# Fixed homes, by their address, for the split weights of a two-layer trunk on one core

## The chip, the cores and the metric

One Trainium2 chip, one core. The time is that of one execution in device microseconds (us). The engines are called PE (TensorE), DVE (VectorE), ACT (ScalarE), POOL (GpSimd) and SP (SyncE, which issues nearly all transfers).

## What is computed

Two layers on x of 512 tokens by 1024 channels, all in float32. Each layer is SwiGLU half-step, mixer, SwiGLU half-step; every sub-layer has a norm, a shift and scale from a conditioning vector, and a gated residual. Layer 0 mixes by gated convolutions, layer 1 by pooling and block attention. Cut to what matters here:

```python
def swiglu(h, w_gate, w_up, w_down):
    return (jax.nn.silu(h @ w_gate) * (h @ w_up)) @ w_down

for i in range(DEPTH):
    mod = (cond @ ada_w[i] + ada_b[i]).reshape(bn, N_SUBLAYERS, 3, D_MODEL)
    h = modulate(rms_norm(x, ffn_norm[i, 0]), mod[:, 0, 0], mod[:, 0, 1])
    x = x + 0.5 * mod[:, 0, 2][:, None, :] * swiglu(h, ...)
    h = modulate(rms_norm(x, mix_norm[i]), mod[:, 1, 0], mod[:, 1, 1])
    x = x + mod[:, 1, 2][:, None, :] * (conv_mixers(h, ...) if i % 2 == 0 else pool_moba_mixers(h, ...))
    h = modulate(rms_norm(x, ffn_norm[i, 1]), mod[:, 2, 0], mod[:, 2, 1])
    x = x + 0.5 * mod[:, 2, 2][:, None, :] * swiglu(h, ...)
return rms_norm(x, final_norm)
```

## The kernel before

Everything is kept transposed: channels on the 128 partitions, the 512 tokens along the free dimension. Each float32 operand of a product is split into a high and a low part of the type float32r, and a product of weights w and stream s is three matmuls: high w with high s, high w with low s, low w with high s (`mac`, lines 302 to 304). The streams are hh and hl (the normed input) and th and tl (the hidden values), eight tiles of 512 columns each.

Weights come from HBM by SP into `raw`, a ring of four tiles. `split` (lines 270 to 294) rounds a block of 128 x 1024 into `whi` on ScalarE (line 284) and puts the rest into `wlo`, mostly on VectorE (line 286). whi and wlo are rings of four places, one tag each with four buffers. A few items keep their split weights elsewhere: in th and tl at the start (the joined items), in hh and hl in the two output projections of the mixers (`store`).

Part of gate times up of every SwiGLU is done by pairs of 128 channels with seven products of half width instead of eight (`pair_run`, `seventh`, line 791). These have 256 columns. Per pair: a11 and a12 (weights split by `split_full` into whi, wlo; streams hh, hl), s1 and s3 (also whi, wlo; streams are the sums `f`, tiles f0 to f15), s2 and a22 (weights split by `split_half` into qhi, qlo, line 748; streams f) and s4 (weights qhi, qlo; streams hh, hl). Each is 12 matmuls, so a pair has 84, and there are 56 pairs in 11 runs:

```python
mm(p.hi[name][:, kk, :], xh, first and kk == 0)
mm(p.hi[name][:, kk, :], xl)
mm(p.lo[name][:, kk, :], xh)
```

Between two sub-layers stands a boundary (`boundary`): the last two items of the old one and the first three of the new one are done in halves of 256 columns with whi and wlo, while the norm is computed. All other products have 512 columns.

The order on each engine is written out: a plan of steps is replayed, a split stands at most three items ahead of its use, and takes the place in the ring that was used four splits ago. Memory comes from pools. Constants, streams and x lie in one pool, then raw, the ring, small buffers, and `fp`, which is opened anew for a stage and holds f, q, and all temporaries. Where a tile starts follows from the sizes of those ahead of it. `keep1` (line 844) copies a quarter result into p1c, a buffer of its own in fp.

Of the kernel before, what the change touches and what calls it, by code (L numbers as in the profile page):

```python
# [8 lines left out]
F32 = mybir.dt.float32  # L9
F32R = mybir.dt.float32r  # L10
# [4 lines left out]
P = 128  # L15
D = 1024
S = 512
# [10 lines left out]
W_BUFS = 4  # L28
# [6 lines left out]
class Raw:  # L35


    def __init__(self, shape, src, uses):
        self.shape, self.src, self.uses = shape, src, uses
        self.tile = None  # L40


class Item:


    def __init__(self, raw, cut, shape, post=None, rhs=None, korder=None, store=None):
        self.raw, self.cut, self.shape = raw, cut, shape
        self.post, self.rhs = post, rhs
        self.korder, self.store = korder, store
        self.hi = self.lo = self.ps = None  # L50
        self.left = 0
        self.pool_low = self.late = self.hold = self.by_dma = False


class Pair:
# [13 lines left out]
class Trunk:  # L69
    def __init__(self, ctx, tc, a, out):  # L70
        self.ctx, self.tc, self.nc, self.a, self.out = ctx, tc, tc.nc, a, out
        self.plan = []
        self.later, self.held = [], []
        self.pend = None
        self.ending = False
        self.phase = None
        self.free_banks = list(range(8))
        self.bank_no = {}

# [173 lines left out]
    def load(self, r):  # L253
# [12 lines left out]
        else:  # L266
            r.tile = t.rearrange("p (a b) -> p a b", a=r.shape[1])
            self.nc.sync.dma_start(r.tile, r.src)

    def split(self, it):  # L270
        nk, m = it.shape
        src = it.cut(it.raw.tile)
        if it.store is None:
            parts = [[p.tile([P, 1024], F32R, name=n, tag=n)[:, 0:nk * m].rearrange(
                "p (a b) -> p a b", a=nk) for p, n in ((self.wp, "whi"), (self.wp, "wlo"))]]
            step = nk
        else:
            parts = [[t.rearrange("p (a b) -> p a b", b=m) for t in pair] for pair in it.store]
            step = S // m
        it.hi, it.lo = [], []  # L280
        for i, (hi, lo) in enumerate(parts):
            w = src[:, i * step:(i + 1) * step, :]
            n = w.shape[1]
            self.nc.scalar.copy(hi[:, 0:n, :], w)  # L284
            eng = self.nc.gpsimd if it.pool_low else self.nc.vector
            low = lambda eng=eng, lo=lo, hi=hi, w=w, n=n: eng.tensor_tensor(  # L286
                lo[:, 0:n, :], w, hi[:, 0:n, :].bitcast(F32), op=ALU.subtract)
            if it.by_dma:
                self.nc.scalar.activation(lo[:, 0:n, :], w, AF.Copy, scale=-1.0)
                self.nc.gpsimd.dma_start(lo[:, 0:n, :], w, accum_op=ALU.add)  # L290
            elif it.hold:
                self.held.append(low)
            else:
                low()
            it.hi += [hi[:, a, :] for a in range(n)]
            it.lo += [lo[:, a, :] for a in range(n)]
# [45 lines left out]
    def setup(self):  # L342
        ctx, tc, nc, a = self.ctx, self.tc, self.nc, self.a
# [4 lines left out]
        self.np_ = ctx.enter_context(tc.tile_pool(name="np", bufs=2))  # L348
        self.psum = ctx.enter_context(tc.tile_pool(name="psum", bufs=1, space=PS))
        ctx.enter_context(tc.manual_schedule())  # L350
        cp = self.cp
        self.open_phase()
        rows = lambda n, c, name, i: self.fp.tile([P, S], F32, name=name, tag=SPARE[9 + i], bufs=1)[0:n, 0:c]
# [101 lines left out]
    def open_phase(self):  # L455
        if self.phase is not None:
            self.phase.close()
        self.phase = ExitStack()
        self.fp = self.phase.enter_context(self.tc.tile_pool(name="fp", bufs=2))


    def g_of(self, l, s):
# [104 lines left out]
    def apply(self, i, k, sl, rb):  # L567

        nc = self.nc
        n = sl.stop - sl.start  # L570
        if n == S:
            t = self.fp.tile([P, n], F32, name=f"t{n}", tag="qhi", bufs=3)
        else:
            t = self.np_.tile([P, n], F32, name=f"t{n}", tag="t", bufs=3)
        nc.vector.scalar_tensor_tensor(t, self.x[k][:, sl], self.modA[:, i, k:k + 1],  # L575
                                       rb, op0=ALU.mult, op1=ALU.mult)
        b = self.modB[:, i, k:k + 1]
        nc.scalar.activation(self.hh[k][:, sl], t, AF.Identity, bias=b, scale=1.0)  # L578
        self.low()
        self.pend = lambda: nc.vector.scalar_tensor_tensor(  # L580
            self.hl[k][:, sl], t, b, self.hh[k][:, sl].bitcast(F32), op0=ALU.add, op1=ALU.subtract)

    def low(self):
        fn, self.pend = self.pend, None
        if fn is not None:
            fn()

    def boundary(self, tail, i, head, switch=True):
# [13 lines left out]
        two, third, fourth = head[:2], head[2:3], head[3:4]  # L602
        third[0].late = fourth[0].late = True
        third[0].pool_low = True
        nk = tail[0].shape[0]
        for it in tail:
            self.mm(it, 0)
# [136 lines left out]

    def split_half(self, p, name, src):

        hi, lo = (self.fp.tile([P, S], F32R, name=n, tag=n, bufs=3) for n in ("qhi", "qlo"))
        self.nc.scalar.copy(hi, src)  # L748
        p.hi[name], p.lo[name] = hi.rearrange("p (k c) -> p k c", k=4), lo.rearrange("p (k c) -> p k c", k=4)
        p.lows = getattr(p, "lows", {})  # L750
        p.lows[name] = lambda: self.nc.vector.tensor_tensor(lo, src, hi.bitcast(F32), op=ALU.subtract)  # L751

    def split_full(self, p, names, src):

        hi, lo = (self.wp.tile([P, 1024], F32R, name=n, tag=n) for n in ("whi", "wlo"))
        self.nc.scalar.copy(hi, src)
        for e, n in enumerate(names):
            p.hi[n], p.lo[n] = (t[:, e * S:(e + 1) * S].rearrange("p (k c) -> p k c", k=4) for t in (hi, lo))
        p.lows = getattr(p, "lows", {})
        p.lows[names] = lambda: self.nc.vector.tensor_tensor(lo, src, hi.bitcast(F32), op=ALU.subtract)  # L760
# [63 lines left out]
    def pair_run(self, pairs, down, rest):  # L824
# [16 lines left out]
                self.plan.append(("use", slot))  # L841

        def keep1(p):
            p.p1 = self.fp.tile([P, 256], F32, name="p1c", tag="p1c", bufs=1)
            nc.scalar.copy(p.p1, p.ab[:, 0:256])

        def u2(p):
# [27 lines left out]
        for n, p in enumerate(pairs):  # L875
# [11 lines left out]
            else:  # L887
                self.pre([down[0]])
            product(p, "s2", "x", 2, True)
            do((keep1, p))  # L890
            if r:
                do((low(r, ("a11", "a12")),))
# [30 lines left out]
        p, nf = pairs[-1], down[0].shape[0]  # L923
# [623 lines left out]
    def build(self):  # L1547
        self.setup()
        self.sg, self.rb = {}, {}
        f = {(l, s): self.ffn_items(l, s) for l in range(2) for s in (0, 2)}  # L1550
# [129 lines left out]
        tail = f[1, 2][-1][1][6:]  # L1680
        self.call(lambda: setattr(self, "ending", True))
        self.call(lambda: self.scaled(range(5), FULL))
        for it in tail:
            self.mm(it, 0)
        nk = SECTIONS[-1]
        for k in range(nk):
# [95 lines left out]
```

## Time and profile before

| what | us |
|---|---|
| median of 3 runs | 1842.7 |
| lowest, highest | 1841.34, 1845.09 |
| the profiled execution | 1845.38 |
| its span, first to last instruction | 1843.6 |
| PE, PEld (its weight loads) busy | 1794.6, 1563.4 |
| DVE, ACT, POOL busy | 1411.1, 816.1, 144.5 |

The profile is of one execution, 1.8 us of which lie outside the span. PEld are the weight loads, which overlap the matmuls. A matmul is recorded from its start to a modelled end, beyond the start of the next one: for how long a product holds up the next, one looks at the distance of starts.

### The profile page before, as it was taken

The page shows a single profiled execution, that of the slowest core. Times are in us where ns is not written, and L with a number is a line of the kernel's source. Part 1 is how long each engine was busy: PE and PEld are TensorE (multiplying, and loading weights), DVE is VectorE, ACT ScalarE, POOL GpSimd, SP SyncE. Part 2 cuts the span into 40 slices and gives each one's busy share as a digit, 9 for nine tenths or more (in the row PEclk, how much of TensorE's full clock was granted, in tenths as well). Part 3 has the DMA queues.
Part 4 walks back from the last instruction along what each step waited for, and adds up shares of the span by engine and source line. Part 5 has one row for each costly group of instructions (what it writes and reads, how often), then busy time and mean ns, then how long its engine had stood idle before and what let it go on. Part 6 is the DMA issues. An engine that isn't in the chain of part 4 may idle for free.

```text
span 1843.6 us, 26711 instructions
## 1 busy us (share of the span) xinstructions
PE 1794.6 (97%) x10730; PEld 1563.4 (85%) x10730; DVE 1411.1 (77%) x2084; ACT 816.1 (44%) x1404; POOL 144.5 (8%) x123
## 2 busy tenths in 40 slices
PE   5999999999999999999999999999999999999998
PEld 3787889988778888989888889998866788898997
DVE  6689879775797869799677787886898586485874
ACT  4322325447754433436344234453545444253543
POOL 2100000005760000000000000000002000000000
PEclk7999999999999999999999999999999999999999
DMA  9585564447752346353423664543462132424321
GB/s 253 164 295 205 172 187 122 138 115 164 166 177 88 115 162 196 123 148 105 160 71 113 218 210 136 145 133 97 134 205 71 54 92 69 114 81 126 92 92 46
DMA packets 275940, 255.93 MB, mean 139 GB/s; under 512 B 5628, under 2 KB 254312, under 8 KB 275816
## 3 DMA queue, kind: packets, MB, share of 16 engines
q1 hardware_dynamic: 273380, 245.78, 43.5%
q0 software_dynamic: 2304, 8.39, 2.5%
q8 instruction: 84, 1.38, 0.3%
q14 instruction: 40, 0.33, 0.1%
q10 hardware_dynamic: 132, 0.05, 0.0%
HBM read 243.72 MB, written 2.10 MB: 133 GB/s over the span
## 4 chain that ended last, share of the span: by engine, by line
PE 81%; DVE 10%; ACT 3%; issue 2%; POOL 2%; DMA 1%; SPq 0%; ACTq 0%; POOLq 0%; DVEq 0%
PE bank L791 30%; PE bank L302 16%; PE bank L304 16%; PE bank L303 16%; DVE hl L580 1%; DVE wlo L286 1%; DVE adaacc L487 1%; DMA raw<-in_ada_w_dram 1%; ACT whi L284 1%; DVE t L575 1%; POOL y L1124 1%; DVE pm L1362 1%; DVE x L1010 1%; DVE p L1359 0%; DVE acc L1524 0%
## 5 line engine op out<-in xcount | busy, mean ns | idle before, releaser
L302 PE MATMUL bank<-th,whi 128*128 128x512 f32 (+1 forms) x896 | 336.6, 376 | 0.7 <-ACT th L1404 0.7
L304 PE MATMUL bank<-th,wlo 128*128 128x512 f32 (+1 forms) x896 | 333.9, 373 | 2.7 <-POOL wlo L286 2.7
L303 PE MATMUL bank<-tl,whi 128*128 128x512 f32 (+1 forms) x896 | 333.4, 372 | 1.1 <-DVE tl L687 0.9
L302 PE MATMUL bank<-hh,whi 128*128 128x512 f32 (+1 forms) x864 | 322.1, 373 | 5.5 <-ACT hh L578 3.2
L303 PE MATMUL bank<-hl,whi 128*128 128x512 f32 (+1 forms) x864 | 316.6, 366 | 8.1 <-DVE hl L580 8.1
L304 PE MATMUL bank<-hh,wlo 128*128 128x512 f32 (+1 forms) x864 | 315.8, 366 | 3.2 <-DVE wlo L286 2.6
L284 ACT CAST whi<-raw 128x1024 fp32r<-128x1024 f32 (+1 forms) x205 | 204.4, 1012 | 135.8 <-PE bank L303 83.3
L286 DVE TENSOR_TENSOR wlo<-raw,whi 128x1024 fp32r<-128x1024 f32 (+1 forms) x179 | 209.4, 1187 | 19.1 <-ACT whi L284 18.4
L304 PEld LDWEIGHTS bank<-th,wlo 128*128 128x128 f32 x896 | 169.4, 189 | 36.1 <-POOL wlo L286 4.3
L303 PEld LDWEIGHTS bank<-tl,whi 128*128 128x128 f32 x896 | 169.6, 189 | 32.3 <-DVE tl L687 1.3
L302 PEld LDWEIGHTS bank<-th,whi 128*128 128x128 f32 x896 | 169.6, 189 | 32.0 <-ACT th L1404 0.9
L303 PEld LDWEIGHTS bank<-hl,whi 128*128 128x128 f32 x864 | 163.4, 189 | 37.9 <-DVE hl L580 9.6
L302 PEld LDWEIGHTS bank<-hh,whi 128*128 128x128 f32 x864 | 163.6, 189 | 36.9 <-ACT hh L578 3.3
L304 PEld LDWEIGHTS bank<-hh,wlo 128*128 128x128 f32 x864 | 163.7, 189 | 33.2 <-DVE wlo L286 3.7
L1010 DVE SCALAR_TENSOR_TENSOR x<-bank,modG,x 128x512 f32<-128x512 f32 (+1 forms) x124 | 85.7, 698 | 133.2 <-PE bank L304 132.3
L791 PE MATMUL bank<-f,qhi 128*128 128x256 f32 x896 | 165.3, 282 | 0.0
L791 PE MATMUL bank<-f,whi 128*128 128x256 f32 x896 | 163.0, 280 | 0.2
L748 ACT CAST qhi<-raw 128x512 fp32r<-128x512 f32 x168 | 100.7, 621 | 111.9 <-issue 77.1
L487 DVE SCALAR_TENSOR_TENSOR adaacc<-raw,cond,adaacc 128x1024 f32<-128x1024 f32 x112 | 143.7, 1283 | 2.7
L791 PEld LDWEIGHTS bank<-f,whi 128*128 128x128 f32 x896 | 137.6, 188 | 1.9 <-ACT yy L851 0.9
L791 PEld LDWEIGHTS bank<-f,qhi 128*128 128x128 f32 x896 | 138.7, 190 | 0.0
L791 PE MATMUL bank<-f,qlo 128*128 128x256 f32 x448 | 126.5, 282 | 0.2 <-DVE qlo L751 0.2
(247 smaller groups left out, 3334.8 us busy)
## 6 DMA issues: line engine op xcount, KB each, us to landing
raw<-in_ada_w_dram SPq DMA_DIRECT2D x64, 1024.0 KB, 5.0
raw<-in_ffn_w_down_dram SPq DMA_DIRECT2D x32, 1024.0 KB, 5.5
raw<-in_ffn_w_gate_dram SPq DMA_DIRECT2D x58, 512.0 KB, 4.1
raw<-in_ffn_w_up_dram SPq DMA_DIRECT2D x58, 512.0 KB, 5.3
raw<-in_ffn_w_gate_dram SPq DMA_DIRECT2D x15, 1024.0 KB, 5.4
raw<-in_ffn_w_up_dram SPq DMA_DIRECT2D x15, 1024.0 KB, 5.4
raw<-in_ffn_w_down_dram SPq DMA_DIRECT2D x16, 768.0 KB, 4.4
raw<-in_conv_w_in_dram SPq DMA_DIRECT2D x20, 512.0 KB, 5.9
```

Source lines behind the costliest of these rows:

```text
L284: self.nc.scalar.copy(hi[:, 0:n, :], w)
L286: low = lambda eng=eng, lo=lo, hi=hi, w=w, n=n: eng.tensor_tensor(lo[:, 0:n, :], w, hi[:, 0:n, :].bitcast(F32), op=ALU.subtract)
L302: nc.tensor.matmul(ps, lhsT=it.hi[k], rhs=xh[:, sl], start=start, stop=False)
L303: nc.tensor.matmul(ps, lhsT=it.hi[k], rhs=xl[:, sl], start=False, stop=False)
L304: nc.tensor.matmul(ps, lhsT=it.lo[k], rhs=xh[:, sl], start=False, stop=stop)
L487: nc.vector.scalar_tensor_tensor(acc, r.tile[:, j, :], self.cond[:, k:k + 1], acc, op0=ALU.mult, op1=ALU.add)
L575: nc.vector.scalar_tensor_tensor(t, self.x[k][:, sl], self.modA[:, i, k:k + 1], rb, op0=ALU.mult, op1=ALU.mult)
L580: self.pend = lambda: nc.vector.scalar_tensor_tensor(self.hl[k][:, sl], t, b, self.hh[k][:, sl].bitcast(F32), op0=ALU.add, op1=ALU.subtract)
L748: self.nc.scalar.copy(hi, src)
L791: mm = lambda w, x, start=False: nc.tensor.matmul(ps, lhsT=w, rhs=x, start=start, stop=False, skip_group_check=True)
L1010: nc.vector.scalar_tensor_tensor(self.x[d][:, sl], ps[:, sl], self.modG[:, i, d:d + 1], self.x[d][:, sl], op0=ALU.mult, op1=ALU.add)
L1124: nc.gpsimd.tensor_tensor(y, y, m, op=ALU.add)
```

## The change

It alters where tiles start in a partition, and nothing in the order: the same instructions stand in the same order on all five engines, with the same tiles apart from their homes. Starts are counted in bytes, modulo 128. The streams hh, hl, th and tl start at 32 in both kernels. The distance of a product is the start of its weights minus that of its stream.

| tiles | start before | start in the change |
|---|---|---|
| hh, hl, th, tl | 32 | 32 |
| whi, wlo in products of 512 columns | 96 | 32 |
| whi, wlo in products of 256 columns | 96 | 96 |
| qhi, qlo | 0 | 96 |
| f, m, sg, s13 | 0 | 32 |
| raw | 96 | 96 |

| products (matmuls) | distance before | in the change |
|---|---|---|
| 512 columns, split weights with hh, hl, th, tl (3984) | 64 | 0 |
| 512 columns, weights in th, tl, hh, hl (168) | 0 | 0 |
| 256 columns, hh and hl with whi, wlo in pairs: a11, a12 (1344) | 64 | 64 |
| 256 columns, f with whi, wlo: s1, s3 (1344) | 96 | 64 |
| 256 columns, f with qhi, qlo: s2, a22 (1344) | 0 | 64 |
| 256 columns, hh and hl with qhi, qlo: s4 (672) | 96 | 64 |
| 256 columns in boundaries, whi, wlo (1296) | 64 | 64 |

For that, each of the ring's four places becomes a tag of its own with one buffer of 1040 elements, laid out at the start (`w_place`); a place is 4160 bytes, so that the places start by turns at 96 and 32, and the view into it begins 0 or 16 elements (64 bytes) in, as the item is `narrow` (256 columns) or not. fp begins 32 bytes later (`skip_bytes`), and the three buffers each of qhi and qlo lie between two fillers of 64 bytes (`place_q`). p1c moves to the small buffers, where it takes turns with the boundary's t in three buffers. ScalarE's copy into p1c so loses a wait for its own engine in 45 of 56 cases.

```diff
--- before.py
+++ after.py
@@ -49,7 +49,7 @@
         self.korder, self.store = korder, store
         self.hi = self.lo = self.ps = None
         self.left = 0
-        self.pool_low = self.late = self.hold = self.by_dma = False
+        self.pool_low = self.late = self.hold = self.by_dma = self.narrow = False
 
 
 class Pair:
@@ -74,6 +74,7 @@
         self.pend = None
         self.ending = False
         self.phase = None
+        self.w_count = 0
         self.free_banks = list(range(8))
         self.bank_no = {}
 
@@ -267,12 +268,20 @@
             r.tile = t.rearrange("p (a b) -> p a b", a=r.shape[1])
             self.nc.sync.dma_start(r.tile, r.src)
 
+    def w_place(self, narrow):
+
+
+        slot = self.w_count % W_BUFS
+        far = (slot % 2 == 0) != narrow
+        self.w_count += 1
+        return [self.wp.tile([P, 1040], F32R, name=n, tag=f"{n}{slot}", bufs=1)[:, 16 * far:16 * far + 1024]
+                for n in ("whi", "wlo")]
+
     def split(self, it):
         nk, m = it.shape
         src = it.cut(it.raw.tile)
         if it.store is None:
-            parts = [[p.tile([P, 1024], F32R, name=n, tag=n)[:, 0:nk * m].rearrange(
-                "p (a b) -> p a b", a=nk) for p, n in ((self.wp, "whi"), (self.wp, "wlo"))]]
+            parts = [[t[:, 0:nk * m].rearrange("p (a b) -> p a b", a=nk) for t in self.w_place(it.narrow)]]
             step = nk
         else:
             parts = [[t.rearrange("p (a b) -> p a b", b=m) for t in pair] for pair in it.store]
@@ -348,6 +357,9 @@
         self.np_ = ctx.enter_context(tc.tile_pool(name="np", bufs=2))
         self.psum = ctx.enter_context(tc.tile_pool(name="psum", bufs=1, space=PS))
         ctx.enter_context(tc.manual_schedule())
+        for n in ("whi", "wlo"):
+            for slot in range(W_BUFS):
+                self.wp.tile([P, 1040], F32R, name=n, tag=f"{n}{slot}", bufs=1)
         cp = self.cp
         self.open_phase()
         rows = lambda n, c, name, i: self.fp.tile([P, S], F32, name=name, tag=SPARE[9 + i], bufs=1)[0:n, 0:c]
@@ -457,6 +469,21 @@
             self.phase.close()
         self.phase = ExitStack()
         self.fp = self.phase.enter_context(self.tc.tile_pool(name="fp", bufs=2))
+        self.q_placed = False
+        self.skip_bytes("pad0", 32)
+
+    def skip_bytes(self, name, n):
+
+        self.fp.tile([P, n // 4], F32, name=name, tag=name, bufs=1)
+
+    def place_q(self):
+
+        if not self.q_placed:
+            self.q_placed = True
+            self.skip_bytes("pad1", 64)
+            for n in ("qhi", "qlo"):
+                self.fp.tile([P, S], F32R, name=n, tag=n, bufs=3)
+            self.skip_bytes("pad2", 64)
 
 
     def g_of(self, l, s):
@@ -569,6 +596,7 @@
         nc = self.nc
         n = sl.stop - sl.start
         if n == S:
+            self.place_q()
             t = self.fp.tile([P, n], F32, name=f"t{n}", tag="qhi", bufs=3)
         else:
             t = self.np_.tile([P, n], F32, name=f"t{n}", tag="t", bufs=3)
@@ -602,6 +630,8 @@
         two, third, fourth = head[:2], head[2:3], head[3:4]
         third[0].late = fourth[0].late = True
         third[0].pool_low = True
+        for it in tail + head[:3]:
+            it.narrow = True
         nk = tail[0].shape[0]
         for it in tail:
             self.mm(it, 0)
@@ -744,6 +774,7 @@
 
     def split_half(self, p, name, src):
 
+        self.place_q()
         hi, lo = (self.fp.tile([P, S], F32R, name=n, tag=n, bufs=3) for n in ("qhi", "qlo"))
         self.nc.scalar.copy(hi, src)
         p.hi[name], p.lo[name] = hi.rearrange("p (k c) -> p k c", k=4), lo.rearrange("p (k c) -> p k c", k=4)
@@ -752,7 +783,7 @@
 
     def split_full(self, p, names, src):
 
-        hi, lo = (self.wp.tile([P, 1024], F32R, name=n, tag=n) for n in ("whi", "wlo"))
+        hi, lo = self.w_place(True)
         self.nc.scalar.copy(hi, src)
         for e, n in enumerate(names):
             p.hi[n], p.lo[n] = (t[:, e * S:(e + 1) * S].rearrange("p (k c) -> p k c", k=4) for t in (hi, lo))
@@ -841,7 +872,7 @@
                 self.plan.append(("use", slot))
 
         def keep1(p):
-            p.p1 = self.fp.tile([P, 256], F32, name="p1c", tag="p1c", bufs=1)
+            p.p1 = self.np_.tile([P, 256], F32, name="t256", tag="t", bufs=3)
             nc.scalar.copy(p.p1, p.ab[:, 0:256])
 
         def u2(p):
@@ -1681,6 +1712,7 @@
         self.call(lambda: setattr(self, "ending", True))
         self.call(lambda: self.scaled(range(5), FULL))
         for it in tail:
+            it.narrow = True
             self.mm(it, 0)
         nk = SECTIONS[-1]
         for k in range(nk):
```

## Rows read from the trace of the kernel before

**Rows 1.** The page, busy shares and 40 slices of the span (tenths)
```profile
PE 1794.6 (97%) x10730; PEld 1563.4 (85%) x10730; DVE 1411.1 (77%) x2084; ACT 816.1 (44%) x1404; POOL 144.5 (8%) x123
...
PE   5999999999999999999999999999999999999998
...
DVE  6689879775797869799677787886898586485874
```

**Rows 2.** The page, chain that ended last, share of the span by engine
```profile
PE 81%; DVE 10%; ACT 3%; issue 2%; POOL 2%; DMA 1%; SPq 0%; ACTq 0%; POOLq 0%; DVEq 0%
```

**Rows 3.** PE by form: out<-stream,weights, count | busy us, mean ns | idle before
```profile
L302 PE MATMUL bank<-th,whi 128*128 128x512 f32 x704 | 282.0, 401 | 0.7 <-ACT th L1404 0.7
...
L302 PE MATMUL bank<-hh,whi 128*128 128x512 f32 x624 | 253.5, 406 | 4.1 <-ACT hh L578 3.2 <-ACT whi L284 0.9
...
L791 PE MATMUL bank<-f,qhi 128*128 128x256 f32 x896 | 165.3, 282 | 0.0
L791 PE MATMUL bank<-f,whi 128*128 128x256 f32 x896 | 163.0, 280 | 0.2
...
L791 PE MATMUL bank<-hh,whi 128*128 128x256 f32 x448 | 124.1, 277 | 0.0
...
L791 PE MATMUL bank<-hh,qhi 128*128 128x256 f32 x224 | 62.7, 280 | 0.0
```

**Rows 4.** Matmuls into bank, 614 to 648 us: ns min/median/max, first to last start
```profile
L302 PE MATMUL bank<-hh,whi x49: 394/394/394, 613.8 to 647.4; 128*128 128x512 f32 x49
```

**Rows 5.** The chain, second output projection, weights in hh and hl
```profile
1458.33 0.23 PE bank L303
...
1467.87 0.23 PE bank L303
```

**Rows 6.** Matmuls into bank, first output projection, 561 to 569.5 us
```profile
L302 PE MATMUL bank<-th,hh x13: 389/389/389, 560.8 to 569.0; 128*128 128x512 f32 x13
```

**Rows 7.** The chain, one run of pairs
```profile
815.77 71.58 PE bank L791 x612
```

**Rows 8.** Matmuls into bank in that run, 816 to 887.3 us
```profile
L791 PE MATMUL bank<-f,qhi x120: 277/283/283, 817.0 to 886.9; 128*128 128x256 f32 x120
...
L791 PE MATMUL bank<-hh,whi x56: 276/276/283, 818.4 to 884.0; 128*128 128x256 f32 x56
```

**Rows 9.** Matmuls into bank, a boundary, 570.4 to 577.3 us
```profile
L302 PE MATMUL bank<-th,whi x21: 276/276/279, 570.3 to 577.1; 128*128 128x256 f32 x21
```

**Rows 10.** Matmuls into bank, another boundary, 1469.2 to 1476.6 us
```profile
L302 PE MATMUL bank<-th,whi x21: 281/281/281, 1469.2 to 1476.3; 128*128 128x256 f32 x21
```

**Rows 11.** Busy us (instructions) in stretches; then PEclk, DMA share, GB/s
```profile
477.00:558.00 81.00, 77.63 (x340) 61.12 (x339) 71.92 (x96) 47.61 (x69) 49.69 (x34) 0.96 0.64 179
1310.00:1457.00 147.00, 141.50 (x624) 101.26 (x623) 117.74 (x224) 73.61 (x174) 13.42 (x10) 0.99 0.39 130
815.80:887.30 71.50, 71.50 (x613) 71.50 (x612) 62.63 (x84) 43.34 (x81) 0.00 (x0) 1.00 0.42 124
```

**Rows 12.** The first two of these stretches, PE instructions of line 302 alone
```profile
477.00:558.00 81.00, 39.81 (x95) 0.96 0.64 179
1310.00:1457.00 147.00, 44.30 (x103) 0.99 0.39 130
```

**Rows 13.** PE in order of time at an entry into 256 columns
```profile
1468.61 0.39 PE L304 MATMUL bank<-th,hl 128*128 128x512 f32 x1
1468.84 0.28 PE L302 MATMUL bank<-th,whi 128*128 128x256 f32 x1
```

**Rows 14.** Matmuls into bank, 1477.9 to 1481 us
```profile
L302 PE MATMUL bank<-th,whi x8: 276/276/369, 1477.8 to 1480.5; 128*128 128x256 f32 x8
```

**Rows 15.** DVE and ACT by form, columns as in rows 3
```profile
L751 DVE TENSOR_TENSOR qlo<-raw,qhi 128x512 fp32r<-128x512 f32 x168 | 111.6, 684 | 8.0 <-ACT qhi L748 8.0
...
L867 DVE TENSOR_TENSOR m<-m,sg 128x512 f32<-128x512 f32 x56 | 38.8, 693 | 19.0 <-ACT sg L863 18.7
...
L845 ACT COPY p1c<-bank 128x256 f32<-128x256 f32 x56 | 20.9, 373 | 20.8 <-PE bank L791 20.2 <-ACT whi L756 0.2
```

## The prediction, made before the changed kernel ran

> **What bounds the kernel now.** I began with the page's busy shares and slices. The reader should see TensorE at 97% of the span, nine tenths or more in 38 of 40 slices, and VectorE at 77% [rows 1]. The chain that ended last says the same: 81% PE, 10% DVE [rows 2], so most of this text is about how long one product takes on TensorE. The third view is the list of TensorE's groups with forms kept apart [rows 3]. The reader should compare rows of equal shape: products of 256 columns have 282 ns (f with qhi), 280 (f with whi, hh with qhi) and 277 (hh with whi), products of 512 columns have 394 in one place [rows 4] and 389 in another, where the weights lie in hh and hl [rows 6]. These means differ though the shape is the same. Only the operands, so their homes, differ.
>
> A matmul's recorded time is longer than the step to the next one, since they are pipelined. The step is the price. A group of 512-column products with split weights, 49 of them, every third of an unbroken series, starts from 613.8 to 647.4 us: 33.6 us / 144 = **233.3 ns** a step, and each has a record of 394 ns [rows 4]. The block of the output projection with weights in hh and hl (distance 0 from its stream) makes 42 steps in 1467.87 - 1458.33 = 9.54 us, **227.1 ns** [rows 5], record 389 [rows 6]. So record minus step is 162 in both, and I use it to turn records into steps. A run of pairs has 612 products of 256 columns in 71.58 us, **117.0 ns** on average [rows 7]. Inside it, records of 276 mean a step of about 114, 280 to 281 about 118, and 283 about 120 [rows 3, 8]. By distance (table in the section on the change): 64 bytes 114, 96 bytes 117 to 118, 0 bytes 120.
>
> One thing there is not settled by the distance. Boundary products of 256 columns, whose distance is 64 bytes throughout, ran at 276 in one boundary and at 281 in another, for 21 products of each kind without a break [rows 9, 10]: 6.8 us / 60 = 113.3 ns and 7.1 / 60 = 118 ns a step. So at 64 bytes there are **two levels**, 113.3 and about 117.8, and a sequence stays on the one it has.
>
> **The change, part by part.** The sum is made against the profiled execution, 1845.4 us, which is 2.7 us over the median of the runs, 1842.7.
>
> *512 columns, distance 64 to 0.* The groups with split weights count 3 x 704 + 3 x 624 = 3984 products [rows 3]. Each step falls by 233.3 - 227.1 = 6.2 ns, at most 24.7 us. Not all of it reaches the end. In the first of the 40 slices PE is busy half of the time, with few such products yet [rows 1]; in the end of the conv stage it is busy 77.6 of 81 us beside VectorE with 71.9, in attention 141.5 of 147 beside VectorE with 117.7 [rows 11]. Of the first of the three lines that make up a product of split operands, 95 and 103 instructions lie in these two stretches [rows 12]: 198 triplets, some 600 matmuls. For the other 3380, PE follows on itself, and the gain counts in full: 3380 x 6.2 = 21.0 us. Of the 600 I count half: 600 x 6.2 / 2 = 1.9 us. Term: **-22.9 us**. Its bounds: -24.7 if all is on the path, and -11.5 if VectorE takes half.
>
> *256 columns in the runs of pairs, distances 0, 96, 64 to 64 throughout.* The groups of the line of the seven products sum to 2 x 896 + 2 x 448 + 3 x 448 + 3 x 224 = 4704 [rows 3]. PE is busy all of the run, 71.5 of 71.5 us, VectorE 62.6 [rows 11]: every ns counts. Upper end: all 4704 go to the fast level, 4704 x (117.0 - 113.3) = -17.4 us. Lower end: all settle on the slow level, 4704 x (117.8 - 117.0) = +3.8 us; that the products of hh with whi lose more there than those of f with qhi gain is in this difference already. Which end? A sequence enters a run right behind 512-column products, which will now be at distance 0. The trace has one such entry without a wait between: the output projection's last product, then the tail at 64 bytes [rows 13], and that one is the 281 of [rows 10], until the reductions for the norm and the waits beside them, behind which 276 stands [rows 14]. The fast example [rows 9] is at the same place of another sub-layer, but came there past a small product of another kind. Runs of pairs hardly wait, so I take the slow level for two thirds of them and the fast for one: (2 x 3.8 - 17.4) / 3 = **-3.3 us**, with both ends kept for the range.
>
> *256 columns in the boundaries.* Their distance is 64 before and after (1296 products), so nothing is changed on purpose; a change of level in a few blocks moves them by 1296 x 2 ns = 2.6 us to either side, taken as 0.
>
> *The ring's places as buffers of their own, the pads, p1c in the pool of t.* No instruction is added, removed or moved on any engine or queue; a place is still reused four splits later. The copy into p1c, 56 x 373 ns on ScalarE [rows 15], now has three buffers in place of one. ScalarE is busy 43.3 us in a run of 71.5 [rows 11], and PE waits for none of it: 0 us. If ScalarE's slack were gone, it would cost what a p1c copy takes, 0.4 us in a pair, 20 us; nothing in the rows points there.
>
> *Other engines' operands* move by 32 to 96 bytes too. On VectorE, an operation of 128x512 takes 684 ns with its operands raw and qhi 32 bytes apart, and 693 with m and sg at the same remainder [rows 15]: at most 9 ns, and VectorE is not the bound there. 0 us.
>
> **Sum:** -22.9 - 3.3 = -26.2, so 1819.2 for an execution like the profiled one, **1816.5 us** against the median.
>
> **A rule against the change.** Rows of one shape differ by 276, 281 and 283, and by 389 and 394 [rows 4, 6, 8]. The Trainium skill, TensorE: Matmul & The Clock Gate, in its step-by-step part, says that TensorE has two independent SBUF read ports and that loading the next weights does not steal read bandwidth from the running matmul. By that rule a home could not matter, and the sum would be 0. The trace does not agree with its plain reading: steps of 227.1 and 233.3 ns stand side by side.
>
> **The rivals.**
> - *All runs of pairs fast.* The first product of a run finds the fast level and keeps it. For it: inside the runs, hh with whi (64 bytes) has a median of 276 [rows 8]. Against it: each comes there from another distance, and the one direct entry from distance 0 is slow. Then -22.9 - 17.4 = -40.3: 1802 us. Chance 0.25.
> - *VectorE takes half of the gain.* Slices with VectorE at nine tenths or more [rows 1] and the stretches of [rows 11] turn PE's gain into waits for tl, hl and wlo; -11.5 for 512 columns, -3.3 or, with every run on the slow level, +3.8 for 256: 1828 us, at the upper end 1835. Against it: in the runs VectorE would be at 62.6 of some 71 us still. Chance 0.18.
> - *Homes don't matter, the operands do.* hh and hl as weights are written long before they are loaded, the split weights just before; the 389 would come from that, or from the stage. Then nothing changes but the noise: 1842.7. Against it: f with qhi, f with whi and hh with whi are all fresh and differ. Chance 0.04. The rule above ends here too.
> - *Slower: distance 0 is bad for fresh weights.* Among 256-column rows distance 0 is the slowest, 283 against 276 [rows 8]. If that holds for 512 columns with split weights, each of the 3380 products loses 7 ns instead of winning 6.2: +23.7, and with -3.3 from the 256 columns 1842.7 + 20.4 = 1863 us. It decides from the point where the record of th with whi at 512 columns is above 394. Against it: the 389 blocks are at distance 0. Chance 0.03.
>
> **How the numbers follow.** The forecast with its own spread (a third to all of the runs slow, 1809 to 1824) has 0.50. The range has to hold 8 in 10: forecast, the fast rival and the typical half-gain are 0.93 with their tails outside, so it goes from 1799, a little below the fast rival, to 1834, near the half-gain's upper end. Measurement can tell about 0.2%, 3.7 us. Faster by more: 0.93, the first three cases. Same: 0.04. Slower: 0.03.
>
> **What would show it.** Right: th with whi and hh with whi at 512 columns with records of 389 where they had 394; f with qhi no longer 283; within one run of pairs all groups on one level, 276 or 281, which says which end of the second term came; 612 products in 69.4 us (fast) or 72.1 (slow). The span of the DVE-paced stretches should fall by under 3 us. Wrong: records of 394 kept, or 512-column records that differ between the ring's places (then the period is not 128 bytes), or new idle time of PE behind VectorE that eats the difference.

## The result, and the profile after

The changed kernel takes 1832.05 us (median of 5 executions, 1827.85 to 1835.02); the kernel before takes 1842.0 beside it. The ratio is 0.9939, 95% interval 0.9922 to 0.9957: faster, by 10 us where 26 were forecast. A second comparison, with its own runs of the kernel before, gave 1829.76 against 1844.79, ratio 0.9924 [0.9911, 0.9937].

The page after, busy times and the chain by engine (before: [rows 1, 2]):

```profile
PE 1782.3 (97%) x10730; PEld 1563.5 (85%) x10730; DVE 1410.1 (77%) x2084; ACT 814.2 (44%) x1404; POOL 145.3 (8%) x123
...
PE 81%; DVE 11%; ACT 3%; issue 2%; POOL 1%; DMA 1%; SPq 0%; POOLq 0%; ACTq 0%; DVEq 0%
```

The bound is what it was. TensorE has 12.3 us less to do, the other engines within 2 us of what they had. TensorE's groups by form, columns as in [rows 3]:

```profile
L311 PE MATMUL bank<-th,whi 128*128 128x512 f32 x704 | 280.1, 398 | 0.7 <-ACT th L1435 0.7
...
L822 PE MATMUL bank<-f,whi 128*128 128x256 f32 x896 | 161.2, 279 | 0.2
L822 PE MATMUL bank<-f,qhi 128*128 128x256 f32 x896 | 161.1, 279 | 0.0
...
L822 PE MATMUL bank<-hh,whi 128*128 128x256 f32 x448 | 125.4, 280 | 0.0
...
L822 PE MATMUL bank<-hh,qhi 128*128 128x256 f32 x224 | 62.6, 279 | 0.0
```

Beside [rows 3], f with qhi falls from 282 to 279, but hh with whi, whose home was not to change, rises from 277 to 280. And th with whi falls from 401 to 398 only, where a fall of 5 to 6 was expected. Four weight blocks in a row, all for products of 512 columns, show why. This is the view of the matmuls into bank (minimum, median, maximum in ns, first and last start), in two stretches that follow each other: ring places 0 and 1, then places 2 and 3.

```profile
L311 PE MATMUL bank<-hh,whi x17: 390/393/404, 611.0 to 622.2; 128*128 128x512 f32 x17
...
L313 PE MATMUL bank<-hh,wlo x16: 390/393/404, 611.5 to 622.0; 128*128 128x512 f32 x16
...
L311 PE MATMUL bank<-hh,whi x17: 389/389/404, 622.2 to 633.1; 128*128 128x512 f32 x17
...
L313 PE MATMUL bank<-hh,wlo x16: 389/389/396, 622.6 to 632.8; 128*128 128x512 f32 x16
```

The weight tiles of the two stretches differ by their places alone, and the records by 4 ns. From the first to the last start of hh with wlo are 45 steps: 10.5 us in the first stretch, 233 ns a step, and 10.2 in the second, 227. I paired the records' starts in the trace with the addresses in the program, step by step, and left out the steps in which TensorE waits. In places 2 and 3 the 512-column step is **227.6 ns**, in 0 and 1 **232.6**, as good as before (233.0). A place is 4160 bytes, so each starts 64 bytes further on than the one ahead of it (modulo 256); with the view's 0 or 64 bytes, weights that are at 0 modulo 128 are at 128 modulo 256 in places 0 and 1 and at 0 in places 2 and 3. **The homes repeat after 256 bytes, not after 128.** Recounted so, the distances are:

| products | before | after |
|---|---|---|
| 512 columns, split weights | 64 | 0 (places 2, 3), 128 (places 0, 1) |
| 256 columns, hh, hl (th, tl) with w | 64 | 64 and 192, half each |
| f with w | 224 | 64 and 192, half each |
| f with q | 0 | 64, a tenth 192 |
| hh, hl with q | 96 | 192 |

The chain's runs of pairs, first one of 444 products in the kernel before (its runs of 612 take 71.58, [rows 7]), then the kernel after:

```profile
722.99 51.95 PE bank L791 x444
```

```profile
283.36 71.77 PE bank L822 x612
719.94 51.55 PE bank L822 x444
811.93 71.07 PE bank L822 x612
...
1164.40 71.07 PE bank L822 x612
1612.74 51.67 PE bank L822 x444
1704.59 71.24 PE bank L822 x612
```

The runs of 612 are neither at the 69.4 nor at the 72.1 us that a run on one level would take.

Executions of one kernel differ by up to 7 us here, and that goes with the granted clock: 0.987 over the span in the profiled execution of 1835.0 us, 0.994 in the one of 1827.9. The windows of the profiled execution (columns as in [rows 11]):

```profile
500.00:540.00 40.00, 36.85 (x154) 28.41 (x154) 34.58 (x46) 25.14 (x37) 28.84 (x18) 0.91 0.55 161
1360.00:1420.00 60.00, 57.50 (x246) 40.25 (x246) 52.66 (x109) 31.82 (x79) 13.41 (x10) 0.94 0.32 100
```

of the same kernel's profile in the second comparison:

```profile
500.00:540.00 40.00, 35.55 (x165) 27.99 (x164) 35.95 (x48) 24.72 (x38) 27.34 (x17) 1.00 0.58 172
1360.00:1420.00 60.00, 56.95 (x255) 39.70 (x253) 51.80 (x111) 32.78 (x82) 13.43 (x10) 1.00 0.32 104
```

and of the kernel before:

```profile
500.00:540.00 40.00, 37.34 (x155) 28.46 (x154) 33.63 (x45) 26.86 (x40) 29.98 (x20) 0.91 0.54 144
1360.00:1420.00 60.00, 56.61 (x249) 39.02 (x250) 53.61 (x105) 30.37 (x75) 13.42 (x10) 1.00 0.31 97
```

In stretches where TensorE waits beside VectorE the first execution was granted 0.91 and 0.94 on average, so it spent some of the time on the 1.2 GHz level, and the second 1.00, 2.4 GHz throughout; the kernel before had 0.91 and 1.00. The clock there differs between executions of one kernel as much as between the kernels. So I read prices from steps, and times only as ratios.

### The profile page after: what moved, and what is told of

Its sections match the earlier page's. It is cut to its first block, busy times and chain, and to the rows that moved or that the text cites. A ratio compares the mean times of both kernels' runs of the same rounds, so it can differ in the third digit from the quotient of the medians.

```text
span 1833.2 us, 26667 instructions
## 1 busy us (share of the span) xinstructions
PE 1782.3 (97%) x10730; PEld 1563.5 (85%) x10730; DVE 1410.1 (77%) x2084; ACT 814.2 (44%) x1404; POOL 145.3 (8%) x123
## 4 chain that ended last, share of the span: by engine, by line
PE 81%; DVE 11%; ACT 3%; issue 2%; POOL 1%; DMA 1%; SPq 0%; POOLq 0%; ACTq 0%; DVEq 0%
PE bank L822 28%; PE bank L311 17%; PE bank L313 17%; PE bank L312 17%; DVE wlo L295 2%; DVE hl L608 1%; DVE adaacc L514 1%; DMA raw<-in_ada_w_dram 1%; DVE t L603 1%; ACT whi L293 1%; DVE pm L1393 1%; DVE acc L1555 1%; DVE x L1041 1%; DVE p L1390 0%; DVE wlo L791 0%
## 5 line engine op out<-in xcount | busy, mean ns | idle before, releaser
L822 PE MATMUL bank<-f,qhi 128*128 128x256 f32 x896 | 161.1, 279 | 0.0
L779 ACT CAST qhi<-raw 128x512 fp32r<-128x512 f32 x168 | 100.5, 619 | 103.9 <-issue 69.4
L584 POOL TENSOR_TENSOR rs<-ms,mhalf 128x2 f32<-128x2 f32 x12 | 8.4, 698 | 1481.8 <-DVE ms L583 1481.8
```

What stands on the lines that cost most here:

```text
L822: mm = lambda w, x, start=False: nc.tensor.matmul(ps, lhsT=w, rhs=x, start=start, stop=False, skip_group_check=True)
```

## The experiments

All distances from here on are modulo 256; where a step is priced, the distance is that of the next weights from the stream that is running. "Steps" are means over all steps without a wait: 512 columns (some 4070), 256 columns of hh, hl, th, tl with w (2559), 256 columns with f or q (3352). The column "by steps" is the sum of count times change of mean, "measured" is the ratio's distance from 1 times the time before in that comparison.

| kernel | 512 | h,w | f/q | us, median | ratio [95%] | by steps | measured |
|---|---|---|---|---|---|---|---|
| before | 233.0 | 114.9 | 118.1 | 1842 to 1845 | | | |
| after | 230.0 | 116.3 | 116.2 | 1832.05 | 0.9939 [0.9922, 0.9957] | -14.8 | -11.2 |
| e1, wide at 0 | 227.4 | 115.8 | 117.8 | 1826.29 | 0.9906 [0.9892, 0.9919] | -21.5 | -17.3 |
| e2, wide at 128 | 232.4 | 115.7 | 117.5 | 1842.90 | 1.0000 [0.9991, 1.0009] | -2.4 | 0 |
| e3, ring alone | 230.1 | 115.5 | 118.3 | 1837.89 | 0.9966 [0.9954, 0.9979] | -9.6 | -6.3 |
| e4, f and q alone | 233.0 | 115.8 | 117.4 | 1845.57 | 1.0010 [1.0001, 1.0019] | 0.2 | 1.8 |
| e5, all at their best | 227.4 | 116.4 | 117.4 | 1826.29 | 0.9903 [0.9889, 0.9917] | -21.1 | -17.9 |
| e6, e1's ring, f and q as before | 227.3 | 114.9 | 118.1 | 1823.64 | 0.9888 [0.9874, 0.9902] | -23.2 | -20.7 |
| e7, ring as before, f and q at 64 | 233.0 | 114.3 | 114.2 | 1832.97 | 0.9944 [0.9930, 0.9958] | -14.6 | -10.3 |
| e8, e5 with the 15 blocks ahead at 64 | 227.9 | 115.8 | 116.8 | 1825.50 | 0.9906 [0.9890, 0.9923] | -23.0 | -17.3 |
| e9, 512 columns at 64, those 15 at 0 | 232.6 | 116.5 | 117.5 | 1845.68 | 1.0008 [0.9999, 1.0017] | 0.7 | 1.5 |
| e10, e5 with first products at 0 | 227.4 | 116.2 | 117.5 | 1825.56 | 0.9894 [0.9877, 0.9910] | -21.4 | -19.5 |
| **e11**, e5 with first f products at 224 | 227.4 | 114.5 | 114.7 | **1812.28** | **0.9830 [0.9816, 0.9844]** | -35.1 | -31.3 |

Where the time falls, it falls by 2 to 6 us less than the steps (by under 1 in the second comparison of the changed kernel). The prediction set aside 1.9 for waits; what makes up the rest is not taken apart here, and executions of one kernel differ by as much (e1: 1823.61 to 1828.99).

Except for e4 and e7, whose ring is the one of before, these kernels have the instructions and the waits of the changed kernel, in the same order on every engine; addresses alone differ.

### Is the period 256? (e1, e2)

The ring's places get sizes and offsets from a table, so that all four have the same homes: 512 columns at 0 (e1) or at 128 (e2), 256 columns of hh, hl, th, tl with w at 64 in both (f with w then lies mostly at 192).

```diff
+PLACES = {"whi": ((1072, 0, 48), (1040, 16, 0), (1072, 0, 48), (1040, 16, 0)), ...
-        far = (slot % 2 == 0) != narrow
...
+            size, *at = PLACES[n][slot]
+            o = at[0] if narrow else at[1]
```

> Every place of the ring puts split weights of 512-column products at the same address modulo 256 as the streams (distance 0), where in the change two places of four stand 128 bytes off; narrow ones stand at 64 in all four. Theory (the homes repeat after 256 bytes, not 128): all 512-column steps near 227.6 ns, as places 2 and 3 have it in the change, none at 232.6; 1930 steps x 5.0 ns = 9.7 us less than the change, about 1822 us. Rival (the two slow places are slow for another reason, their turn in the ring or what is written beside them): places 0 and 1 stay at 232.6 and the time at 1832 us.

> As the first, with 512-column split weights 128 bytes off the streams (modulo 256) in all four places. Theory: all 512-column steps at about 232.6 ns, 2000 steps x 5.0 ns = 10 us more than the change, about 1842 us, as before the change. Rival (the turn in the ring decides): half of the steps stay at 227.6, 1832 us.

TensorE's group of th with whi in e1, then in e2 (before: 401, [rows 3]):

```profile
L314 PE MATMUL bank<-th,whi 128*128 128x512 f32 x704 | 277.6, 394 | 0.7 <-ACT th L1438 0.7
```

```profile
L314 PE MATMUL bank<-th,whi 128*128 128x512 f32 x704 | 281.2, 399 | 0.7 <-ACT th L1438 0.7
```

The two kernels have the same instructions in the same order; moving the weights by 128 bytes is worth 0.0094 of the time. The period is settled from the other side too: in e1 the steps at 0, 256, 512 and 768 modulo 1024, some 1000 each, have means of 227.2 to 227.5 ns. With all places at 0 the 512-column steps sum to what was forecast: 4071 x (233.0 - 227.4) = 22.8 us. The time of e1 is 4 us above what I expected from the change (1822): its f and q steps are at 117.8 ns where the change has 116.2, 5.4 us in 3352.

### The two halves of the change (e3, e4)

e3 keeps the changed ring and puts f and q back; e4 keeps the changed f and q and puts the ring back.

```diff
-        self.q_placed = False
-        self.skip_bytes("pad0", 32)
+        self.q_placed = True
```

```diff
...
+        return [self.wp.tile([P, 1024], F32R, name=n, tag=n) for n in ("whi", "wlo")]
...
```

> The change's ring alone: places as separate buffers with their homes, but f, qhi and qlo start where they did before. Theory (the 512-column products are all of the gain, 3.2 ns x 3984 = 12.6 us by their mean steps, and the second part is worth about nothing): 1829 to 1833 us, within 3 us of the change; f with qhi back at 120 ns, hh with whi nearer 114 than in the change. Rival (moving f and q is worth what the prediction's fast level gave, 8 us or more, and something else eats it): 1838 us or more.

> The other part alone: f, qhi and qlo at their new starts, p1c among the small buffers, the ring as before (all split weights 64 bytes off the streams, 512-column steps at 233.3 ns). Theory (256-column products only change between two levels, f with q gains 3.7 us and hh with whi loses as much): 1838 to 1843 us. Rival (this part is worth the 17 us of an all-fast level when the ring does not disturb it): 1825 us.

In the ring alone the 512-column steps fall by half of what they fall by in e1 (2.9 of 5.6 ns), as the period demands. The time falls by 6.3 us, and 1837.89 is 5 us above the range that I had stated; by steps, 2.2 us of that are 256-column steps that rose. f and q alone give nothing or lose a little (1.0010, above the 1838 to 1843 that I expected): their own steps fall from 118.1 to 117.4 ns, and those of h with w, whose home in e4 is the one of before, rise from 114.9 to 115.8. So the price of a 256-column product is not a matter of its own distance alone.

### A price list (two sweeps)

Each of the four places has its own pair of homes, by other numbers in the table.

> A price list in place: the four places of the ring put split weights of 512-column products 32, 96, 160 and 224 bytes off the streams (modulo 256), those of 256-column products at 0, 32, 128 and 160. Theory (the home modulo 256 sets how often the weights' reads meet the stream's): each place has its own 512-column step, all between 226 and 241 ns, and none under that of distance 0 (227) by more than 2 ns; 256-column steps of hh with the ring differ by place too, with two levels, 113.3 and 117.8, at some and only one at others. Rival (only halves of 128 bytes count beside the exact meeting): 32 to 224 all cost 233. Time between 1835 and 1848 us.

> The same with 16, 48, 192 and 240 bytes for 512 columns, and 16, 96, 192 and 224 for 256. Theory: 16 and 240, next to the exact meeting, are no better than 0; 192 lies near 230, as the products of the values with the ring as stream had it before the change (distance 192); 256-column steps of hh with the ring at 192 on two levels as in the change, at 96 and 224 near 117 as f and s4 had there before. Rival: 16 and 240 cost as 0 does, so that lines of 32 bytes are what counts. Time between 1832 and 1848 us.

They had one run each. The first took 1852.89 us, 5 above its range, the second 1839.15, beside 1841.12 for the kernel before. Mean step in ns by distance, from these and the kernels above:

| bytes | 0 | 16 | 32 | 48 | 64 | 96 | 128 | 160 | 192 | 224 | 240 |
|---|---|---|---|---|---|---|---|---|---|---|---|
| 512 columns | 227.4 | 229.9 | 233.1 | 233.1 | 233.2 | 234.0 | 232.6 | 233.4 | 229.4 | 233.1 | 227.8 |
| 256 columns | 119.3 | 117.7 | 118.2 | | 113 or 118 | 117.5 | 118.5 | 119 | 113 or 118 | 117.2 | 119.0 |

For 512 columns, 0 and 240 stand out, 16 and 192 lie half-way, and the others are within 1.4 ns of one another. For 256, 64 and 192 were seen on 113 ns through whole stretches, 64 more often (means of 115.7 against 116.9 in the changed kernel); the others' means hide uneven steps.

### Every product at its best home (e5, e6, e7)

e5 is e1 with f and q moved on so that all 256-column products are at 64, but some 260 at 0, in the first two runs of pairs. e6 is e1's ring with f and q as before. e7 is the ring as before (64 for everything) with f and q at 64.

```diff
-        self.skip_bytes("pad0", 32)
+        self.skip_bytes("pad0", 160)
...
-            self.skip_bytes("pad2", 64)
```

> Every 512-column product's next weights start at 0 modulo 256 bytes from its stream, and every 256-column product's at 64 except some 260 at 0. Theory (the price of a step is set by that distance alone): 512-column steps 227.4 ns as in the first ring experiment; 256-column steps 115.5 ns in all four kinds of pair, where the f and q pairs took 117.8, so 3350 x 2.2 ns = 7 us less than that experiment: 1819 us (1815 to 1822). Rival (the run of a pair program sits on one of two levels whatever the homes are): 256-column steps at 117 to 118, time 1824 to 1828 us, as the ring alone.

> The ring of the first ring experiment (512 columns at 0, 256 at 64 in all four places) with the f and q tiles as they were before the change. Theory: 512-column steps 227.4 ns; h,w steps at 64: 115 ns; f,q at 0 back at 119.4, f,w at 224 at 117, h,q at 96 at 117.5, in the sum what the f and q pairs took before: 1826 to 1829 us. Rival (the part on f and q is worth 5 us, as the run of the changed ring without it suggests): 1831 us or more.

> The ring as before the change (every distance of w 64), f and q placed so that f,q, f,w and h,q are at 64 as well. Theory: 512-column steps 233 ns as before; f and q pairs from 118.1 to 115.5 ns, 3350 x 2.6 = 8.7 us less, h,w as before at 115: 1834 us (1832 to 1837). Rival (what f and q gain the other products give back, as when f and q alone were moved as in the change): 1841 to 1845 us.

> The changed kernel once more, on the same chip as the three beside it, for a comparison: 1832 us (1828 to 1835), 0.994 of the kernel before; 512-column steps at 227.6 and 232.6 ns by ring place, as in its first profile. A theory in which the two levels are a matter of the run would have them mixed otherwise.

The changed kernel came out as it had (1829.76 us, steps of 227.6 and 232.6 by place). e7 is right to about 1 us, and e5, which has the same distances in its 256-column products, misses by 7 us and comes out as its rival had it. The chain's runs of pairs in e5:

```profile
804.51 72.08 PE bank L824 x612
...
1155.37 72.08 PE bank L824 x612
```

and in e7:

```profile
812.20 69.36 PE bank L813 x612
...
1164.62 69.37 PE bank L813 x612
```

The matmuls into bank within one of these runs, e5 and then e7:

```profile
L824 PE MATMUL bank<-f,qhi x120: 281/281/281, 805.8 to 876.2; 128*128 128x256 f32 x120
...
L824 PE MATMUL bank<-hh,whi x56: 281/281/281, 807.2 to 873.3; 128*128 128x256 f32 x56
```

```profile
L813 PE MATMUL bank<-f,qhi x120: 276/276/276, 813.4 to 881.2; 128*128 128x256 f32 x120
...
L813 PE MATMUL bank<-hh,whi x56: 276/276/276, 814.8 to 878.3; 128*128 128x256 f32 x56
```

Minimum, median and maximum agree: a run at 64 is wholly on one level or wholly on the other. These are the two levels of [rows 9, 10]. (The first run of 612, which holds most of the products at 0, takes 71.1 us in e5, e7 and all kernels below, and is on neither.) What differs between the two kernels is the ring: its 512-column products, those right ahead of a run among them, are at 0 in e5 and at 64 in e7. e6, with worse homes for f and q than e5, is no slower, since its uneven f and q products leave the h, w products on the fast level (114.9 against 116.4).

### What sets the level? (e8 to e11)

A 512-column step with the next weights at 0 takes 226 to 227 ns nearly throughout; at 64, most steps take 231 and 236 ns by turns (in some stretches, that of [rows 4] among them, all take 233 to 234). e8 is e5 with the fifteen weight blocks of 512-column products that stand right ahead of a stretch of 256 columns at 64; e9 is the mirror image, those fifteen at 0 and all other 512-column products at 64.

```diff
+ENTRY = (28, 40, 62, 102, 114, 134, 156, 170, 186, 202, 224, 260, 272, 292, 314)
...
+        narrow = narrow or self.w_count in ENTRY
```

> As the kernel with every distance at its best (512 columns at 0, 256 at 64), but the one 512-column product that stands right ahead of each stretch of 256-column products (15 of some 170, 325 records) is at 64 too. Theory (a stretch of 256-column products at 64 has two levels, 113 and 118 ns, and keeps the one that the 512-column steps ahead of it leave it on): the pair runs of 612 go from 72.1 to 69.4 us and those of 444 from 52.3 to 50.3 us, as in the kernel whose 512-column products were all at 64; 5870 steps x 2.8 ns = 16 us less and 325 x 5.7 ns = 2 us more than 1826: 1812 us (1809 to 1816). Rival (the level comes from the ring's places, which differ between those two kernels): pair runs stay at 72.1 us, 1826 to 1829 us.

> The mirror image in the same ring: 512-column products at 64 except the 15 right ahead of the stretches, which are at 0; 256-column products at 64. Theory (the level is handed over by the product ahead): pair runs at 72.1 us though everything in them and nearly all around them is as in the kernel where they took 69.4; 512-column steps 233 ns: 1826 + 3600 x 5.7 ns = 1846 us (1843 to 1849). Rival (what counts is the distance inside the run, or the ring at large): pair runs at 69.4 us, 1831 to 1835 us.

e9 is as expected, to the us: one block ahead at 0, and the runs that took 69.4 us in e7 take 72.1:

```profile
815.34 72.08 PE bank L826 x612
...
1171.25 72.08 PE bank L826 x612
```

e8 misses: of the nine runs of pairs that are wholly at 64 only one went over. The chain in e8:

```profile
803.16 72.08 PE bank L826 x612
...
1154.62 69.37 PE bank L826 x612
```

PE in order of time at these two entries (start, us, line, tiles; two equal instructions share a row):

```profile
802.53 0.40 PE L317 MATMUL bank<-tl,whi 128*128 128x512 f32 x1
802.77 0.39 PE L318 MATMUL bank<-th,wlo 128*128 128x512 f32 x1
803.00 0.40 PE L826 MATMUL bank<-f,whi 128*128 128x256 f32 x2
...
1153.99 0.39 PE L317 MATMUL bank<-tl,whi 128*128 128x512 f32 x1
1154.22 0.40 PE L318 MATMUL bank<-th,wlo 128*128 128x512 f32 x1
1154.46 0.39 PE L826 MATMUL bank<-f,whi 128*128 128x256 f32 x2
```

The last step ahead is 0.23 us in the first, 0.24 in the second (231 and 236 ns in the records): the turns of 231 and 236 end on the other foot. In e5, e7, e8 and e9 there are 44 entries into a longer stretch at 64 without a wait between. In 33 the last step took 225 to 231 ns, and the stretch is slow; in 11 it took 233 to 236, and the stretch is fast. The entries whose last step was one of 368 to 373 ns, with a small product of another kind between, are fast too, 16 of 16. A wait inside a stretch at 64 leads to either level, though: behind 116 of them in these four kernels 76 go on fast and 40 slow, so [rows 14] is one case and not the rule.

Can that be had with all 512-column products at 0? e10 puts the weights of a stretch's first product (in a run of pairs 12 matmuls) at 0, e11 those of a run's first f product at 224.

```diff
+FIRST = (30, 42, 104, 116, 136, 172, 188, 204, 247, 262, 274, 294, 315)
...
+        narrow = narrow and self.w_count not in FIRST
```

```diff
+FIRST = (30, 42, 104, 116, 136, 172, 188, 204, 262, 274, 294)
...
+            o = 40 if first else at[0] if narrow else at[1]
```

> The kernel with 512 columns at 0 and 256 columns at 64 everywhere, but the weights of the first product of 13 stretches of 256-column products are at 0 (some 300 records). In the records so far a stretch at 64 starts on 113 ns where the step ahead of it took 235 ns or more, or 119 to 120 ns, and on 118 ns where it took 225 to 231 ns or 118 ns, and then keeps it; products of 256 columns at 0 have steps of 119 to 120 ns and were followed by 113 in 45 of 45 cases. Theory (the last step ahead sets the level): the first product takes 119 ns, and from the second on the stretch is on 113: pair runs of 612 at 69.5 us instead of 72.1, of 444 at 50.5 instead of 52.3; 3400 records x 4.4 ns = 15 us less, 300 x 2 ns more: 1812 us (1809 to 1816). Rival (a stretch that began on 118 falls back to it, as it did after the products moved to 64 ahead of the stretches): pair runs at 72.1 us, 1825 to 1828 us.

> The same kernel (512 columns at 0, 256 at 64), with the weights of the first f product of 11 stretches at 224 instead of 0. In the kernel with the ring alone a product at 224 ahead of one at 64 ended on 120, 117 ns and was followed by 114, 113, 113 in 11 of 11 cases, although the stretch had begun on 118; its steps are uneven (113 to 120) where those at 0 are all 120. Theory (uneven steps shift the phase that a stretch at 64 keeps): pair runs of 612 at 69.5 us, of 444 at 50.5 us, 3000 records x 4.4 ns = 13 us less than 1826: 1813 us (1810 to 1817). Rival (a stretch entered from 512 columns at 0 falls back to 118, as it did with the first product at 0): pair runs at 72.1 us, 1824 to 1828 us.

In e10 the entry step is 226 to 227, the first product then runs on even steps of 119 to 121 ns, and behind it the stretch falls back to 118:

```profile
805.57 72.10 PE bank L826 x612
```

A step of 119 to 121 ns ahead is not enough. The 45 cases of its expectation had one step at 224 between the products at 0 and those at 64; e10 has none. In e11 the entry steps are 235, then 118, 117, 116, 118, 120, 113, 116, 117, 120, 114, 116, and from there 113 and 114 to the end. The chain in e11:

```profile
711.45 50.36 PE bank L826 x444
801.83 69.40 PE bank L826 x612
...
1150.76 69.40 PE bank L826 x612
1594.44 50.36 PE bank L826 x444
1684.55 69.40 PE bank L826 x612
```

and its page:

```profile
PE 1758.1 (97%) x10730; PEld 1550.0 (86%) x10730; DVE 1408.6 (78%) x2084; ACT 813.5 (45%) x1404; POOL 145.1 (8%) x123
```

e11 takes 1812.28 us, 0.983 of the kernel before: the same instructions in the same order as the change, 17 to 20 us below what the change took in its two comparisons, by homes alone. Whether the 235 ns at its head or the uneven steps behind it bring the level is not told apart; in e6 uneven steps of a product at 224 did it 11 times of 11 with no long step ahead, in the kernel before 10 times of 11.

## Why the prediction was right and wrong

- **What bounds the kernel**: right. TensorE is at 97%, the chain at 81% PE, and each kernel's change of time follows its mean steps to within 6 us.
- **512 columns, -22.9 us: the step that failed.** The prediction has "each step falls by 233.3 - 227.1 = 6.2 ns" for all 3984 products. It holds at 0 modulo 256, where the 227.1 of [rows 5] was read; half of the changed ring's places are at 128, where a step is 232.6. 4071 x (233.0 - 230.0) = 12.2 us is what was there to win. The size per step was right (e1: 227.4, 22.8 us), the count was half: 10.7 of the 15 us that are missing from the forecast 26.2. The table of distances modulo 128 was taken from the change's own terms, and the rows that were read could not refute it: their split weights were all at one distance. The trace of before held a hint all the same. Where whi and wlo are the stream and hh and hl the weights, the distance is 192, which modulo 128 is 64 again, and 73 such steps without a wait have a mean of 229.8 ns, against 233.2 for the split weights at 64. The prediction named the sign of it ("records that differ between the ring's places"), but gave it no chance of its own and no price; half of the term, 11 us, could have been put on it.
- **256 columns in the runs, -3.3 us**: the net is near, but by luck, since the way to it is not the one that was forecast. The f and q products won 3352 x 1.9 = 6.4 us, and the h, w products in the runs, half of them moved to 192, rose from 114.3 to 117.6 ns and lost 1340 x 3.4 = 4.5: together -1.9. "To 64 throughout" did not come about, so neither did a run on one level. The two levels themselves, and that a stretch behind 512 columns at 0 starts on the slow one, were read rightly from [rows 9, 10, 13]: e5 shows it in all eleven such entries. Of the runs of which the prediction took a third as fast, none is fast in e5.
- **Boundaries, 0 us**: nearly right. Half of their products moved to 192 as well, and their mean step went from 115.5 to 114.9 ns, 0.8 us less in 1219 steps; the 1.4 ns that h, w lose in the table are lost in the runs.
- **Buffers, p1c, other engines, 0 us**: right as far as it shows; DVE went from 1411.1 to 1410.1 us and ACT from 816.1 to 814.2, and e2, which has all of this, takes the time of the kernel before (1.0000). No run changes p1c alone.
- **The rule against the change** (the Trainium skill, TensorE: Matmul & The Clock Gate, on two independent read ports) would have left the time as it was. e1 and e2 differ in nothing but homes, by 16.6 us; the measurement decides against its plain reading.
- **The rivals**: all runs fast (1802) needed homes that the change does not have; it came true in e11 in part. VectorE taking half (1828) would give nearly the time that was measured, for a reason that the runs do not bear out: e6 and e1 have the full 512-column gain beside the same VectorE and keep all but 2.5 to 4 us of it. That distance 0 is bad for fresh weights fell with e1, and that the operands decide and not their homes fell with e1 against e2.

## What to carry to other kernels

Where TensorE bounds a kernel and rows of one shape differ by a few ns, pair the records' starts with the addresses of stream and next weights before choosing homes, and take the period from data: a sweep with a different distance per buffer costs one run and shows it. A best home for each product by itself is not yet the best kernel (e5): look at what the level of a long stretch is, and at the last steps ahead of it. And where a change rests on a stated remainder, ask which rows of the profile would look the same if that remainder were twice as large.

## What I had not expected of the hardware

- The step between matmuls depends on where the next weights lie against the stream, with a period of 256 bytes: 227.4 ns at 0 against 232.6 at 128 for 512 columns (e1, e2), and in the other direction for 256 columns, 119.3 at 0 against 113 to 118 at 64.
- A stretch of 256-column products at 64 keeps the level it starts on, 113.3 or 117.8 ns a step, through 612 products, past changes of weights, streams and banks; at an entry without a wait what stands ahead decides it (33 slow and 11 fast of 44 by the last step; e9 against e7). What inside the engine does that, no run here shows.
- At 64, 512-column steps mostly take 231 and 236 ns by turns rather than their mean, and which of the two comes last is what the next stretch's level goes with (e8).
